# Short-sequence attention on one core: output held in SBUF until unit 34, four q and k buffers, the v wait on ScalarE, a placed loop head

## The chip, the cores and the metric

The kernel runs on one core of a Trainium2 chip. Time is device time in microseconds (us). The kernel before has a median of 143.16 us over nine runs. One execution was profiled: it took 142.82 us, of which the profile's span covers 140.7 us.

## The reference

There are 32 x 12 = 384 heads, each of sequence length 128 and head size 64, all float32.

```python
scale = 1.0 / np.sqrt(q.shape[-1])
scores = scale * np.matmul(q, k.transpose(0, 1, 3, 2))
scores_max = np.max(scores, axis=-1, keepdims=True)
attn = np.exp(scores - scores_max)
attn = attn / (np.sum(attn, axis=-1, keepdims=True) + 1e-8)
return np.matmul(attn, v).astype(np.float32)
```

q, k and v are drawn with a standard deviation of 0.1, so the scores are small and the kernel takes the exponential without subtracting the maximum.

## The kernel before, in words

The heads form 48 units of eight. Four units share one load of q and one of k (a "super", 12 in all) and one load of v (a "group", 12 in all). Each load reads 1 MiB of float32 and lands in SBUF as 512 KiB of bf16. The cast is made by the DMA, and all 36 loads are issued by GpSimd in one fixed order (`pool_load`): v of a group, then q and k of the next super.

TensorE runs a loop of seven trips over eight steps each (`tensor_program`). A step u has up to four parts: T, the transposes that bring q and k into head-major form; V, the matmuls with a selection matrix that put v's rows in order; S, the scores of unit u + 1; and O, the values of unit u. Unit m of v is reordered at step m - 3. The first and last trips skip the parts whose unit doesn't exist, with a branch on the trip number. Code outside TensorE is unrolled.

Between them the other engines work as follows. VectorE makes the pair tile for a transpose two steps ahead (P, `pair_up`), copies the transposed result out of PSUM (E, `keep_qk`) and normalises (N: a reciprocal and a multiply that writes `o_sb`). In a step its order is N, E, P. ScalarE copies each reordered v out of PSUM with a column of ones beside it (K, `keep_v`), then takes the exponentials (X, `exps`). SyncE issues the stores in order of the units. Everything is ordered by semaphores: each operation lists what it depends on, and a wait is placed in front of it.

Four places matter for the change.

- **The stores.** Output goes through ten buffers (`NO`), each of two units. Store c waits until the unit 14 after its last is normalised, but never beyond unit 36 (`LATE`, `LOADED`, line 373). The normalise that reuses a buffer waits for the store that used it ten before (line 346). Most stores are two DMAs.
- **The q and k buffers.** There are eight of each (`NQ`). A load waits for the pairs that read the buffer it overwrites (line 389).
- **The wait for v.** There are two v buffers (`NVB`), so group g may be issued only when the last unit of group g - 2 has been reordered (line 379). The landing of a group is waited for by VectorE, at the pair tile made for the step of the group's first reorder (line 330). TensorE's reorder in turn waits for that pair tile (line 297), and for the ScalarE copy of the unit before.
- **The loop head.** The loop on TensorE starts wherever the code ahead of it ends (line 493).

```python
        last = first + n - 1
        op("SP", ("store", c), emit, [("N", max(last, min(last + LATE, LOADED)))])
```

Of the kernel before, what the change touches and what calls it, by code (L numbers as in the profile page):

```python
# [10 lines left out]
def kernel(  # L11
# [7 lines left out]
    nc = tc.nc  # L19
    f32 = mybir.dt.float32  # L20
# [3 lines left out]
    B, H, S, D = q.shape  # L24
# [7 lines left out]
    NU = B * H // 8  # L32
# [32 lines left out]

    PERIOD = 8
    TRIPS = NU // PERIOD + 1


# [7 lines left out]
        v_at[m - 3] = [m]  # L79
    steps = range(min(t_at) - 2, NU + 1)  # L80

    NQ, NVB, NVE, NP, NT, NA, NO = 8, 2, 8, 4, 2, 4, 10

    LATE, LOADED = 14, NU - 12

    def sb(name, shape, dtype):
        return ctx.enter_context(nc.sbuf_tensor(name, shape, dtype))
# [11 lines left out]
    pair = [sb(f"pair{i}", [128, 8, 2, D], bf16) for i in range(NP)]  # L99
    qkT = [sb(f"qkT{i}", [128, 2, 16, S], bf16) for i in range(NT)]  # L100
    attnT = [sb(f"attnT{i}", [128, 2, 4, S], bf16) for i in range(NA)]
    o_sb = [sb(f"o_sb{i}", [128, 2 * 2 * RO * D], f32) for i in range(NO)]
    recip = [sb(f"recip{i}", [128, 2, RO], f32) for i in range(2)]
    qk_ps = ps("qk_ps", [128, 8 * S], bf16)
    s_ps = [ps(f"s_ps{i}", [128, 2, 4 * S], f32) for i in range(2)]
# [17 lines left out]
    def op(engine, key, emit, deps=(), marks=(), dma=()):  # L123
        o = Op()
        o.key, o.emit, o.deps, o.marks, o.dma = key, emit, deps, marks, dma
        assert key not in position, key
        position[key], engine_of[key] = len(program[engine]), engine
        program[engine].append(o)
# [101 lines left out]
    def keep_v(m):  # L230
        return nc.scalar.copy(v_e[m % NVE][:, :, :D], v_ps[:].rearrange("p (n e) -> p n e", e=D))  # L231
# [27 lines left out]
    def normalise(u):  # L259
        c, w, n, first = splace[u]  # L260
        o4 = o_ps[:, :, :RO * (D + 1)].rearrange("p a (r e) -> p a r e", e=D + 1)
        r = recip[u % 2]
        nc.vector.reciprocal(r[:], o4[:, :, :, D]).then_inc(s_r, 1)  # L263
        nc.vector.wait_ge(s_r, u + 1)
        o = o_sb[c % NO][:, :n * 2 * RO * D].rearrange("p (a w e) -> p a w e", a=2, w=n)
        return nc.vector.tensor_mul(  # L266
            o[:, :, w, :].rearrange("p a (r d) -> p a r d", d=D),
            o4[:, :, :, :D],
            r[:].unsqueeze(3).to_broadcast([128, 2, RO, D]))
# [6 lines left out]
    s_q = [tc.alloc_semaphore(f"s_q{i}") for i in range(NQ)]  # L276
    s_k = [tc.alloc_semaphore(f"s_k{i}") for i in range(NQ)]
    s_v = [tc.alloc_semaphore(f"s_v{i}") for i in range(NVB)]
    s_o = [tc.alloc_semaphore(f"s_o{i}") for i in range(NO)]
    v_readers = {}  # L280
    for u in range(NU):
        for a in range(2):
# [10 lines left out]

    def pe_order_v(m):

        g, w, n, first = vplace[m]
        deps = [("K", m - 1)] + ([("P", t_at[vstep_of[m]][0])] if w == 0 else [])
        op("PE", ("V", m), lambda: order_v(m), deps, ["pe_act"])

    def pe_scores(u):  # L300
        s = of_unit[u]
# [5 lines left out]
    def pe_values(u):  # L307
# [2 lines left out]
        deps.append(("N", u - 1))  # L310
        op("PE", ("O", u), lambda: values(u), deps, ["pe_dve"])

    def act_keep(m):
        deps = [("V", m)]
        if m >= NVE:
            deps += [("O", u) for u in v_readers[m - NVE]]
        op("ACT", ("K", m), lambda: keep_v(m), deps, ["act_pe"])

    def act_exps(u):
        deps = [("S", u)] + ([("O", u - NA)] if u >= NA else [])  # L320
# [2 lines left out]
    def dve_pair(t):  # L323
        s, j, b = t
        deps = [("T", t_order[t_index[t] - NP])] if t_index[t] >= NP else []
        dma = [((s_q, s_k)[j][s % NQ], 16 * (s // NQ + 1))]
        for m in v_at.get(t_step[t], []):
            g, w, n, first = vplace[m]
            if w == 0:
                dma.append((s_v[g % NVB], 16 * (g // NVB + 1)))  # L330
        op("DVE", ("P", t), lambda: pair_up(t), deps, ["dve_io"] if t_index[t] else ["dve_pe", "dve_io"], dma)

    def dve_keep(t):
# [7 lines left out]

    def dve_normalise(u):
        c, w, n, first = splace[u]
        dma = []
        if w == 0 and c >= NO:
            dma.append((s_o[c % NO], sum(16 * pieces(x) for x in range(c % NO, c, NO))))

        marks = ["dve_pe"] + (["dve_io"] if u + 8 > t_step[t_order[-1]] else [])
        op("DVE", ("N", u), lambda: normalise(u), [("O", u)], marks, dma)

    def pieces(c):

        first = sum(stores[:c])
        return 2 if 1 < stores[c] < supers[of_unit[first]][0] // 4 else 1

    def sp_store(c):
        n = stores[c]
        first = sum(stores[:c])
        R, f = supers[of_unit[first]]
        J = R // 4  # L360

        def emit():
            dst = o_rows[:, 2 * f:2 * f + 2 * J, :].rearrange("p (a w) e -> p a w e", a=2)[
                :, :, first - f:first - f + n, :]
            src = o_sb[c % NO][:, :n * 2 * RO * D].rearrange("p (a w e) -> p a w e", a=2, w=n)
            if pieces(c) == 1:
                nc.sync.dma_start(out=dst, in_=src).then_inc(s_o[c % NO], 16)
            else:
                for a in range(2):
                    nc.sync.dma_start(out=dst[:, a], in_=src[:, a]).then_inc(s_o[c % NO], 16)  # L370

        last = first + n - 1
        op("SP", ("store", c), emit, [("N", max(last, min(last + LATE, LOADED)))])

    def pool_load(kind, x):
        deps = []
# [19 lines left out]
        op("POOL", ("load", kind, x), emit, deps)  # L396


    op("ACT", ("K", -1), lambda: nc.scalar.drain(), [], ["act_pe"])
    at_step = {}  # L400
    for u in steps:
        start = len(program["PE"])
# [68 lines left out]
    def tensor_program():  # L471

        ops, waits, when = {}, {}, {}
        for o in program["PE"]:
            place = at_step[o.key] % PERIOD, o.key[0]
            w = waits_of("PE", o)
            assert waits.setdefault(place, w) == w and not o.dma, (o.key, w, waits[place])
            when.setdefault(place, []).append((at_step[o.key] // PERIOD + 1, o.emit is None))
            if at_step[o.key] // PERIOD == 2:
                ops[place] = o  # L480
        places = []
        for place in [(l, kind) for l in range(PERIOD) for kind in "TVSO"]:
            trips = [t for t, empty in when[place] if not empty]
            assert trips in (list(range(TRIPS - 1)), list(range(1, TRIPS))), (place, trips)
            waiting = len(when[place]) > len(trips)
            assert not waiting or len(when[place]) == TRIPS
            skipped = 0 if trips[0] else TRIPS - 1
            if waiting or not places or places[-1][0] != skipped:
                places.append((skipped, waits[place] if waiting else [], []))
            places[-1][2].append((ops[place], [] if waiting else waits[place]))  # L490
        trip = ctx.enter_context(nc.tensor.register("trip"))
        nc.tensor.reg_mov(trip, 0)
        with nc.tensor.Fori(0, TRIPS):
            for skipped, always, some in places:
                run_waits("PE", always)
                with nc.tensor.If_ne(trip, skipped):
                    for o, w in some:
                        run("PE", o, w)
            nc.tensor.reg_add(trip, trip, 1)

    with nc.Block() as block:
        @block.gpsimd
        def _(_e):
            for i, o in enumerate(program["POOL"]):
                if i == 2:
                    nc.gpsimd.wait_ge(s_zero, 1)
                    nc.gpsimd.affine_select(  # L507
                        out=ident[:], in_=ident[:], compare_op=mybir.AluOpType.not_equal,
                        fill=1.0, base=0, pattern=[[-1, 128]], channel_multiplier=1,
                    ).then_inc(s_id, 1)  # L510
                run("POOL", o, waits_of("POOL", o))

        @block.tensor
        def _(_e):
            tensor_program()

        @block.scalar
        def _(_e):
            for o in program["ACT"]:
                run("ACT", o, waits_of("ACT", o))  # L520

        @block.vector
        def _(_e):
            for t in sel.values():
                nc.vector.memset(t[:], 0.0)  # L525
            nc.vector.memset(ident[:], 0.0).then_inc(s_zero, 1)
            for t in v_e:
                nc.vector.memset(t[:, :, D:D + 1], 1.0)
            nc.vector.wait_ge(s_id, 1)

            for jv in range(2):
                nc.vector.tensor_copy(  # L532
                    sel[16][:].rearrange("p h v (x y s) -> p h v x y s", x=2, y=2)[:, :, jv, :, jv, :],
                    ident[:].rearrange("p (h s x) -> p h x s", h=8, x=2))
            for o in program["DVE"]:
                run("DVE", o, waits_of("DVE", o))

        @block.sync
        def _(_e):
            for o in program["SP"]:  # L540
                run("SP", o, waits_of("SP", o))
            for i in range(NO):
                nc.sync.wait_ge(s_o[i], sum(16 * pieces(x) for x in range(i, len(stores), NO)))


# [28 lines left out]
```

## Time and profile before

| what | value |
|---|---|
| median of the runs | 143.16 us (142.47 to 148.13) |
| profiled execution, its span | 142.82 us, 140.7 us |
| TensorE matmul busy | 99.3 us (71%) |
| VectorE busy | 90.1 us (64%) |
| ScalarE busy | 74.3 us (53%) |
| GpSimd's DMA queue (loads) | 18.88 MB, 76.8% of 16 engines |
| SyncE's DMA queue (stores) | 12.59 MB, 28.2% of 16 engines |
| instruction fetch of one queue | 4 transfers, 0.07 MB |
| granted TensorE clock, mean | 0.914 |

The DMA figures count bytes on the SBUF side. Packets overlap on an engine, so a share can be over 1. A busy row for TensorE overlaps its own weight loads. A wait is listed with the engine and tile that ended it; "issue" is idle time for which the profile shows no wait, and "PEq" is TensorE's sequencer.

### The profile page before, as it was taken

The numbers are of one execution on the slowest core, as the hardware profiler recorded it, in microseconds if no ns is written. First come the engines' busy times: TensorE is split into PE (matmuls) and PEld (weight loads), VectorE is DVE, ScalarE is ACT, GpSimd is POOL, SyncE is SP. The second block draws the span as 40 slices with busy tenths as digits, with TensorE's granted clock in tenths as the row PEclk, the third lists the DMA queues.
The fourth block names the chain that finished last, engine by engine and source line by source line (L and its number), as shares of the span: only waits on it lengthen the run. The fifth ranks groups of instructions, "written<-read, shape, count | busy, mean of one in ns | idle before, by whom it ended". The sixth has DMA issues, their size and how long they took to land. (4 is left out here: it accounts for less than half of the span.)

```text
span 140.7 us, 6998 instructions
## 1 busy us (share of the span) xinstructions
PE 99.3 (71%) x3072; PEld 70.1 (50%) x3072; DVE 90.1 (64%) x204; ACT 74.3 (53%) x97; POOL 27.0 (19%) x41
## 2 busy tenths in 40 slices
PE   0052939999859799885896797797694498597410
PEld 0042626677646566653574574475463366465310
DVE  2143623999599597965874973964964785685640
ACT  3000207778748848676357278077373448469700
POOL 6910002305060320602302302301500200000000
PEclk9999995999999999999779789689999959999955
DMA  2999999899999999999999999999999999999981
GB/s 17 187 201 211 208 206 177 138 200 183 178 184 160 212 186 192 209 180 236 243 235 239 251 237 240 252 235 242 253 231 240 255 226 311 379 373 369 327 302 61
DMA packets 25928, 31.55 MB, mean 224 GB/s; under 512 B 1345, under 2 KB 19777, under 8 KB 25921
## 3 DMA queue, kind: packets, MB, share of 16 engines
q0 software_dynamic: 12864, 18.88, 76.8%
q1 hardware_dynamic: 13056, 12.59, 28.2%
q8 instruction: 4, 0.07, 0.2%
q14 instruction: 4, 0.02, 0.0%
HBM read 37.75 MB, written 12.58 MB: 358 GB/s over the span
## 5 line engine op out<-in xcount | busy, mean ns | idle before, releaser
L231 ACT CAST v_e<-v_ps 128x512 bf16<-128x512 f32 x48 | 28.2, 588 | 57.7 <-PE v_ps L185 57.7
L236 ACT ACTIVATE attnT<-s_ps 128x1024 bf16<-128x1024 f32 x48 | 49.4, 1029 | 0.3 <-PE s_ps L211 0.2
L171 PE MATMUL qk_ps<-ident,pair 128*128 128x128 bf16 x384 | 33.4, 238 | 15.8 <-PEq L458 15.0
L254 DVE COPY qkT<-qk_ps 128x1024 bf16<-128x1024 bf16 x48 | 32.8, 684 | 4.6 <-PE qk_ps L171 3.5
L171 PEld LDWEIGHTS qk_ps<-ident,pair 128*128 128x128 bf16 x384 | 25.0, 106 | 20.8 <-issue 19.5
L185 PE MATMUL v_ps<-v_b,sel 128*32 128x256 bf16 x768 | 33.2, 297 | 2.9 <-issue 2.1
L266 DVE TENSOR_TENSOR o_sb<-o_ps,recip 128x512 f32<-128x512 f32 x48 | 33.2, 692 | 1.7
L223 PE MATMUL o_ps<-v_e,attnT 128*32 128x65 bf16 x1536 | 21.9, 202 | 16.5 <-PEq L458 16.3
L223 PEld LDWEIGHTS o_ps<-v_e,attnT 128*32 128x32 bf16 x1536 | 16.2, 101 | 22.6 <-issue 19.9
L381 POOL DMA_DIRECT2D v_b<-in_v_dram x12 | 9.5, 788 | 82.2 <-PE v_ps L185 82.2
L245 DVE COPY pair<-k_b 128x1024 bf16<-128x1024 bf16 x24 | 10.7, 446 | 20.0 <-DMA v_b<-in_v_dram 20.0
L185 PEld LDWEIGHTS v_ps<-v_b,sel 128*32 128x32 bf16 x768 | 17.2, 101 | 9.7 <-issue 4.9
L211 PE MATMUL s_ps<-qkT 64*128 64x128 bf16 x384 | 20.5, 231 | 0.6 <-PEq L458 0.5
L263 DVE RECIPROCAL recip<-o_ps 128x8 f32<-128x8 f32 x48 | 9.8, 203 | 13.2 <-PE o_ps L223 7.8
L211 PEld LDWEIGHTS s_ps<-qkT 64*128 64x128 bf16 x384 | 11.7, 99 | 11.6 <-issue 11.6
L245 DVE COPY pair<-q_b 128x1024 bf16<-128x1024 bf16 x24 | 10.4, 433 | 3.7 <-DMA q_b<-in_q_dram 3.6
L393 POOL DMA_DIRECT2D q_b<-in_q_dram x12 | 8.7, 724 | 1.0 <-SPq L92 1.0
L393 POOL DMA_DIRECT2D k_b<-in_k_dram x12 | 8.9, 738 | 0.0
L231 ACT ACT_TABLE_LOAD x1 | 1.3, 1283 | 1.0 <-SPq L92 1.0
L532 DVE COPY sel<-ident 128x128 bf16<-128x128 bf16 x2 | 0.4, 224 | 1.7 <-POOL ident L507 1.7
L525 DVE MEMSET sel<- 128x256 uint32 x1 | 0.3, 272 | 1.1 <-SPq L92 1.1
L507 POOL TENSOR_SCALAR_AFFINE_SELECT ident<-ident 128x128 bf16<-128x128 bf16 x1 | 0.3, 313 | 0.1
(6 smaller groups left out, 0.8 us busy)
## 6 DMA issues: line engine op xcount, KB each, us to landing
out_dram<-o_sb SPq DMA_DIRECT2D x48, 256.0 KB, 7.1
q_b<-in_q_dram POOLq DMA_DIRECT2D x12, 512.0 KB, 11.4
k_b<-in_k_dram POOLq DMA_DIRECT2D x12, 512.0 KB, 13.6
v_b<-in_v_dram POOLq DMA_DIRECT2D x12, 512.0 KB, 9.8
```

The costliest lines, as they stand in the source:

```text
L171: i = nc.tensor.transpose(p[:, :, r4, jj, :], x[:, r].rearrange("p a d -> p (a d)"), ident[:])
L185: x = nc.tensor.matmul(t[r4 * 32:(r4 + 1) * 32, i, :, :], lhsT=pick[:, w * nh + i, jv, :], rhs=v_b[g % NVB][:, :n, (4 * jv + r4) * D:(4 * ...
L211: i = nc.tensor.matmul(t[:, a, h, :], lhsT=x[p, 1, 4 * w + h, :], rhs=x[p, 0, 4 * w + h, :], start=True, stop=True)
L223: y = nc.tensor.matmul(t[h * SO:(h + 1) * SO, a, r * (D + 1):(r + 1) * (D + 1)], lhsT=x[:, a, h, r * SO:(r + 1) * SO], rhs=v_e[m % NVE][:, ...
L231: return nc.scalar.copy(v_e[m % NVE][:, :, :D], v_ps[:].rearrange("p (n e) -> p n e", e=D))
L236: return nc.scalar.activation(out=attnT[u % NA][:].rearrange("p a h (r s j) -> p (a h r) s j", r=4, j=J), in_=s_ps[u % 2][:].rearrange("p ...
L245: return nc.vector.tensor_copy(pair[t_index[t] % NP][:], src[:, 8 * b:8 * b + 8])
L254: return nc.vector.tensor_copy(x.rearrange("p h (r j s) -> p (h r) j s", r=4, j=J)[:, :, 2 * b:2 * b + 2, :].rearrange("p x j s -> p x (j ...
L263: nc.vector.reciprocal(r[:], o4[:, :, :, D]).then_inc(s_r, 1)
L266: return nc.vector.tensor_mul(o[:, :, w, :].rearrange("p a (r d) -> p a r d", d=D), o4[:, :, :, :D], r[:].unsqueeze(3).to_broadcast([128, ...
L381: op("POOL", ("load", kind, x), lambda: nc.gpsimd.dma_start(out=v_b[x % NVB][:, :n, :], in_=v_rows[:, first:first + n, :],).then_inc(s_v[x ...
L393: nc.gpsimd.dma_start(out=bufs[x % NQ][:], in_=rows[R][:, n:n + 2, :]).then_inc(sm[x % NQ], 16)
```

## The change

The output buffers become one per store, the whole output in SBUF (26 tiles, 96 KiB per partition). Each store waits for its own last unit or for unit 34, whichever is later, so nothing is stored before unit 34 and then all held stores follow at once. The normalise waits for no store. q and k have four buffers each in place of eight.

The wait for a group of v moves from VectorE to ScalarE. The copy K of the unit before a group's first (for the first group, a drain) now also waits for that group's landing, and TensorE's reorder waits for that copy alone.

The loop on TensorE is built with a set place of its first instruction: slot 108 of a block in which instructions are fetched. The code ahead of it branches over the padding.

```diff
-    PERIOD = 8
+    PERIOD, FIRST = 8, -8
...
-    NQ, NVB, NVE, NP, NT, NA, NO = 8, 2, 8, 4, 2, 4, 10
-
-    LATE, LOADED = 14, NU - 12
+    NQ, NVB, NVE, NP, NT, NA = 4, 2, 8, 4, 2, 4
+
+    HELD = NU - 14
...
-    o_sb = [sb(f"o_sb{i}", [128, 2 * 2 * RO * D], f32) for i in range(NO)]
+    o_sb = [sb(f"o_sb{c}", [128, n * 2 * RO * D], f32) for c, n in enumerate(stores)]
...
-        g, w, n, first = vplace[m]
-        deps = [("K", m - 1)] + ([("P", t_at[vstep_of[m]][0])] if w == 0 else [])
-        op("PE", ("V", m), lambda: order_v(m), deps, ["pe_act"])
+        op("PE", ("V", m), lambda: order_v(m), [("K", m - 1)], ["pe_act"])
...
+    def v_landing(m):
+        if m == NU or vplace[m][1]:
+            return []
+        g = vplace[m][0]
+        return [(s_v[g % NVB], 16 * (g // NVB + 1))]
+
     def act_keep(m):
...
-        op("ACT", ("K", m), lambda: keep_v(m), deps, ["act_pe"])
+        op("ACT", ("K", m), lambda: keep_v(m), deps, ["act_pe"], v_landing(m + 1))
...
-        for m in v_at.get(t_step[t], []):
-            g, w, n, first = vplace[m]
-            if w == 0:
-                dma.append((s_v[g % NVB], 16 * (g // NVB + 1)))
...
-        if w == 0 and c >= NO:
-            dma.append((s_o[c % NO], sum(16 * pieces(x) for x in range(c % NO, c, NO))))
...
-        op("SP", ("store", c), emit, [("N", max(last, min(last + LATE, LOADED)))])
+        op("SP", ("store", c), emit, [("N", max(last, HELD))])
...
-    op("ACT", ("K", -1), lambda: nc.scalar.drain(), [], ["act_pe"])
+    op("ACT", ("K", -1), lambda: nc.scalar.drain(), [], ["act_pe"], v_landing(0))
...
-        with nc.tensor.Fori(0, TRIPS):
+        with nc.Fori(
+                0, TRIPS, engines=bass.OrderedEngineSet([nc.tensor.engine]),
+                head_slot={nc.tensor.engine: 108}):
```

The rest of the diff is bookkeeping that follows from these: semaphores of the stores counted by four, and the trip of a step counted from step -8, which gives the same trips as before.

More of the change, by code (lines that the diff above doesn't have):

```diff
@@ L264, in normalise @@
         nc.vector.wait_ge(s_r, u + 1)
-        o = o_sb[c % NO][:, :n * 2 * RO * D].rearrange("p (a w e) -> p a w e", a=2, w=n)
+        o = o_sb[c][:].rearrange("p (a w e) -> p a w e", a=2, w=n)
         return nc.vector.tensor_mul(
@@ L278 @@
     s_v = [tc.alloc_semaphore(f"s_v{i}") for i in range(NVB)]
-    s_o = [tc.alloc_semaphore(f"s_o{i}") for i in range(NO)]
+    s_o = [tc.alloc_semaphore(f"s_o{i}") for i in range(4)]
     v_readers = {}
@@ L343, in dve_normalise @@
         c, w, n, first = splace[u]
-        dma = []
-        if w == 0 and c >= NO:
-            dma.append((s_o[c % NO], sum(16 * pieces(x) for x in range(c % NO, c, NO))))
         marks = ["dve_pe"] + (["dve_io"] if u + 8 > t_step[t_order[-1]] else [])
-        op("DVE", ("N", u), lambda: normalise(u), [("O", u)], marks, dma)
+        op("DVE", ("N", u), lambda: normalise(u), [("O", u)], marks)
     def pieces(c):
@@ L364, in emit @@
                 :, :, first - f:first - f + n, :]
-            src = o_sb[c % NO][:, :n * 2 * RO * D].rearrange("p (a w e) -> p a w e", a=2, w=n)
+            src = o_sb[c][:].rearrange("p (a w e) -> p a w e", a=2, w=n)
             if pieces(c) == 1:
-                nc.sync.dma_start(out=dst, in_=src).then_inc(s_o[c % NO], 16)
+                nc.sync.dma_start(out=dst, in_=src).then_inc(s_o[c % 4], 16)
             else:
                 for a in range(2):
-                    nc.sync.dma_start(out=dst[:, a], in_=src[:, a]).then_inc(s_o[c % NO], 16)
+                    nc.sync.dma_start(out=dst[:, a], in_=src[:, a]).then_inc(s_o[c % 4], 16)
         last = first + n - 1
-        op("SP", ("store", c), emit, [("N", max(last, min(last + LATE, LOADED)))])
+        op("SP", ("store", c), emit, [("N", max(last, HELD))])
     def pool_load(kind, x):
@@ L474, in tensor_program @@
         for o in program["PE"]:
-            place = at_step[o.key] % PERIOD, o.key[0]
+            trip, l = divmod(at_step[o.key] - FIRST, PERIOD)
+            place = l, o.key[0]
             w = waits_of("PE", o)
             assert waits.setdefault(place, w) == w and not o.dma, (o.key, w, waits[place])
-            when.setdefault(place, []).append((at_step[o.key] // PERIOD + 1, o.emit is None))
-            if at_step[o.key] // PERIOD == 2:
+            when.setdefault(place, []).append((trip, o.emit is None))
+            if trip == 2:
                 ops[place] = o
@@ L541, in _ @@
                 run("SP", o, waits_of("SP", o))
-            for i in range(NO):
-                nc.sync.wait_ge(s_o[i], sum(16 * pieces(x) for x in range(i, len(stores), NO)))
+            for i in range(4):
+                nc.sync.wait_ge(s_o[i], sum(16 * pieces(x) for x in range(i, len(stores), 4)))
 _INS = ['q', 'k', 'v']
```

## The prediction

> **What bounds the kernel now.** I read the slices first, then stages cut at the landings of v, then the waits, then the timeline around one landing. The two rows of the page's slices (40 slices of 3.5 us):
>
> ```profile
> DMA  2999999899999999999999999999999999999981
> GB/s 17 187 201 211 208 206 177 138 200 183 178 184 160 212 186 192 209 180 236 243 235 239 251 237 240 252 235 242 253 231 240 255 226 311 379 373 369 327 302 61
> ```
>
> The DMA engines are full from the second slice to the last but one, yet at three rates: about 200 GB/s while only loads run, 240 with stores among them, 370 with stores alone. So the end is set by transfers. The stages (columns: start and end, us, busy of five engines with counts, clock, DMA share, GB/s):
>
> ```profile
> 4.00:24.00 20.00, 10.71 (x144) 7.16 (x148) 7.38 (x14) 3.33 (x6) 3.98 (x7) 0.92 1.15 207
> 24.00:26.00 2.00, 2.00 (x92) 1.52 (x88) 1.48 (x4) 1.39 (x2) 1.83 (x3) 0.94 0.33 47
> 26.00:38.90 12.90, 12.42 (x444) 9.04 (x428) 10.77 (x25) 10.26 (x15) 2.23 (x3) 1.00 1.11 189
> 38.90:55.70 16.80, 13.76 (x495) 10.00 (x490) 14.26 (x33) 11.76 (x16) 4.36 (x6) 1.00 1.09 185
> 55.70:120.60 64.90, 50.97 (x1561) 35.80 (x1560) 44.45 (x97) 36.70 (x49) 11.90 (x16) 0.89 1.13 242
> 120.60:130.00 9.40, 7.00 (x280) 4.98 (x278) 7.14 (x15) 6.66 (x10) 0.00 (x0) 1.00 1.08 373
> 130.00:138.80 8.80, 2.41 (x128) 1.64 (x112) 3.60 (x8) 2.92 (x3) 0.00 (x0) 0.70 0.83 284
> ```
>
> Three losses are to be seen. At 24 to 26 us the DMA nearly stops (share 0.33). From 26 to 55.7 us loads alone run at 187 (the byte-weighted mean of 189 and 185), where the first eight, all queued at once, ran at 207. From 130 us stores run at 284, not 373, because they wait for the last units. The waits:
>
> ```profile
> POOL v_b L381 <- PE v_ps L185: 82.2, 10, 16.0
> DVE pair L245 <- DMA v_b<-in_v_dram: 20.0, 11, 2.7
> DVE recip L263 <- DMA out_dram<-o_sb: 5.1, 5, 2.2
> ```
>
> GpSimd may issue a group of v only when TensorE has reordered the last unit of the group two before; VectorE waits for each landing; five times it waits for an output buffer. The timeline, at the start and around the landing of the fourth group of v:
>
> ```profile
> 20.26 0.62 PE L185 MATMUL v_ps<-v_b,sel 128*32 128x256 bf16 x15 [2.13 <-issue]
> ...
> 23.68 0.74 POOL L381 DMA_DIRECT2D v_b<-in_v_dram  x1 [16.02 <-PE v_ps L185]
> ...
> 38.94 0.43 DVE L245 COPY pair<-k_b 128x1024 bf16<-128x1024 bf16 x1 [1.84 <-DMA v_b<-in_v_dram]
> 39.07 0.75 POOL L381 DMA_DIRECT2D v_b<-in_v_dram  x1 [5.43 <-PE v_ps L185]
> ...
> 40.35 0.43 PE L223 MATMUL o_ps<-v_e,attnT 128*32 128x65 bf16 x32 [1.27 <-PEq L458]
> ```
>
> TensorE stops 2.13 us in the middle of a reorder, with no semaphore named; the third v is issued at 23.68, as the queue runs dry; at 38.94 VectorE, freed by a landing, lets the values matmul go 1.4 us later.
>
> **The ledger of before.** Loads are 18.88 MB in SBUF (12 groups of q, k, v, 1.573 MB each), stores 12.59 MB. By 55.7 us the rows have moved 4.14 + 0.09 + 2.44 + 3.11 = 9.78 MB of loads; 9.10 remain. The mixed stage moved 64.9 x 242 = 15.7 MB, so 6.6 MB were stores, 17.7 us at the 373 of stores alone; the loads there had 47.2 us, or 193 GB/s. Transfers end near 138.75, the span at 140.7, the profiled execution at 142.82. The median, 143.16, is 0.34 above it; 1% (1.4 us) is about what a measurement of this kernel tells from no change.
>
> **Stores held to unit 34.** Nothing is taken off the DMA: the same 48 stores, 12.59 MB, 33.75 us at 373. [...] By the rows, what can change is how full the engines are when loads run alone (187 against 193), and the slack at the end. In the last 8.8 us 284 x 8.8 = 2.50 MB moved, 6.7 us at 373: 2.1 us of slack. All units will be done long before the last store, so this goes, but for a ragged finish of the DMA engines that I put at 0.7 (0 to 2). The issuing work on SyncE is covered: two issues of one store were 0.41 us apart in the trace, a half store takes 0.35 us at 373, and the queue starts beside loads. If that cover is gone, 27 further issues cost 0.06 each, 1.6 us at most. The five output waits (5.1 us on VectorE) go, and with them five waits of SyncE's issue order; they lay beside loads, so 0.
>
> **q and k in 4 buffers.** q and k of the next super are issued right behind a v that waits for TensorE; the pairs that read the buffer four back were made over ten steps before. Cost 0; the v gate covers it, and if q were gated it would show as a new GpSimd wait on pair.
>
> **The v wait from VectorE to ScalarE.** VectorE's pair at two steps ahead no longer waits for v. Now the copy of the unit before each group waits for the landing, with that step's exponential queued behind it on ScalarE; TensorE stops at the group's first reorder, behind that copy. After a landing: copy 0.59, reorder 0.62, three steps of 1.85 (transposes began at 24.35 and 35.47, six steps), some 0.3 of handoffs: the gate of the next v opens 7.1 us after the landing. In before it took 9.06 and 9.21 (38.94 to the issue at 48.00, 47.62 to 56.83). So each v is issued some 2 us sooner after a landing. With landings 8.2 us apart that is 1.1 us ahead of the next landing rather than 0.1 to 0.4 behind it. The exponential behind the wait ends at 0.1 + 0.59 + 1.03 = 1.7, about when TensorE has passed reorder and scores (1.6), so 0 to 0.2 per group, off the path as long as 7.4 us of compute per group is under the landing interval. What it buys is a deeper queue: bounds are 187 (no better than before alone) and 207 (the queue always deep). I take 191, nearer 187, because not all of the shortfall need be dry queue: the DMA share at 187 was still 1.09 to 1.11.
>
> **The start, and the loop head.** The first k pair no longer waits for the first v (2.69 us on VectorE), so the reorders start near 12.3 instead of 14.09, and are then paced by q at 15.5 and k at about 18. The fourth reorder ends near 20.7 if TensorE doesn't stop, and near 23 if it does. [...] The first trip takes branches over parts whose units don't exist yet. [...] Then v is issued near 21, the lag from issue to flow is about 2 us (23.68, and 47 GB/s until 26), and the stop at 24 to 26 goes: 0.32 MB, 1.5 us, which if kept comes back whole.
>
> **The sum.** Transfers end at 24 + (18.88 - 4.14) MB / r + 33.75 + 0.7. At r = 191 that is 24 + 77.2 + 34.45 = 135.6, 3.1 before 138.75; 142.82 - 3.1 = 139.7 us.
>
> **Rivals.**
> Start stop kept, loads no better than alone before: r = 187, 78.8 us, plus 1.5: 142.8. For it: the unexplained part of 187; against it, two waits ahead of the start are removed. No measurable change.
>
> The queue of loads starves: loads alone lose to the gate on v_b what stores filled in the mixed stage. The place is each switch from k to v between 26 us and the release; the price is r for 14.74 MB. Shorter stages show how low it goes: 176 in 37.5 to 46.1 us. At 176: 83.75 us, 146.3. It is slower than before from r under 184, by over 1% under 180. For it: two thirds of the loads now have no stores beside them. Against it: the 2 us earlier gate.
>
> Held stores crowd out the last loads. Unit 34 comes at about 24 + 11.6 MB / 0.191 + 4.7 = 89, with 2.25 MB of loads left. At 120 GB/s (half of the 242) they take 19 us; the last eight units' compute, 13 us more, is done at 122, 12 before the stores. It decides only where loads get under about 70 GB/s. Stores wholly first would mean about 150. The mixed stage gave loads 9.10 of 15.7 MB, which speaks against it.
>
> Queue always deep: r = 207, 71.2 us, 133.7.
>
> **Chances.** Forecast (r 187 to 197: 141.3 to 137.3) 0.56; start stop kept, no change 0.17; starved loads 0.14; crowded last loads 0.03; deep queue 0.10. Faster by over 1% of the median (under 141.7; r over 186): 0.66; within 1% 0.17; slower 0.17. The range, 136.5 to 145.0, leaves out the ends of starved and deep.
>
> **What would show it.** Slices near 190 GB/s until about 89 us, then a mixed stretch, then 370 to the end; no slice near 138 at 25 us; ScalarE's copies waiting for v, VectorE's pairs not; v issued about 7 us after each landing; no wait on o_sb; the last normalise many us before the last landing. Wrong if loads alone fall under 184 GB/s, if TensorE's stop moves to where v's third issue waits for it, or if pure stores in long runs drop below 373.

## The result and the profile after

The change takes 140.31 us (median of 10 runs, 138.70 to 142.93). The kernel before, run beside it, took 143.36 us (31 runs). The ratio is 0.976, with an interval of 0.972 to 0.980. The forecast was 139.7. Ratios here are of the faster executions alone (those within 1.5% of the fastest of the same kernel), so that a ratio can differ from the quotient of two medians, and the profiled execution of the change, 141.31 us with a span of 139.2, is not among them. Where its rates matter, a row of e1 stands beside it: the change without the placed loop head, an execution of 139.62 us.

The slices of the page of the change (40 slices of 3.5 us):

```profile
DMA  2999999699999999999999999999999999999992
GB/s 16 183 198 211 208 212 189 95 203 176 184 205 143 193 208 211 205 206 213 187 204 182 203 192 210 197 157 214 244 260 374 382 380 377 354 363 349 347 340 91
```

Loads run alone to about 91 us, a short mixed stretch follows, then stores alone. Two things don't fit the forecast: the slice of 95 near 25 us is still there, and the stores fall from 380 to between 340 and 363 in the last five full slices. The stages (columns as for before: start and end, us, busy of five engines with counts, clock, DMA share, GB/s):

```profile
4.00:24.00 20.00, 9.55 (x126) 6.44 (x128) 7.15 (x14) 4.09 (x6) 3.65 (x6) 0.95 1.14 207
24.00:26.00 2.00, 2.00 (x64) 1.58 (x58) 0.98 (x3) 1.43 (x2) 1.85 (x3) 0.65 0.24 36
26.00:91.00 65.00, 61.05 (x2140) 44.11 (x2132) 59.74 (x133) 50.17 (x67) 17.81 (x25) 1.00 1.13 194
91.00:104.00 13.00, 10.71 (x376) 7.72 (x376) 10.84 (x24) 8.79 (x12) 0.74 (x1) 1.00 1.13 219
104.00:120.00 16.00, 10.80 (x399) 7.56 (x392) 8.61 (x18) 9.62 (x12) 0.00 (x0) 0.82 1.09 375
120.00:136.90 16.90, 0.25 (x19) 0.09 (x7) 0.90 (x2) 0.00 (x0) 0.00 (x0) 0.50 1.02 343
```

Loads alone run at 194 GB/s to 91 us; 191 was forecast. The 187 of before is of a shorter stretch, since its stores begin near 55 us. In that stretch the rows of before, of the change and of e1 are:

```profile
26.00:55.70 29.70, 26.18 (x931) 19.04 (x916) 25.03 (x58) 22.01 (x30) 6.59 (x9) 1.00 1.10 187
```

```profile
26.00:55.70 29.70, 27.61 (x972) 19.90 (x960) 27.21 (x61) 22.68 (x30) 6.90 (x10) 1.00 1.11 188
```

```profile
26.00:55.70 29.70, 27.68 (x965) 20.02 (x963) 27.08 (x62) 22.68 (x31) 7.14 (x10) 1.00 1.13 195
```

In this stretch the profiled change gains next to nothing. Its third group of v comes late, and the granted clock was 0.50 from 22.0 to 25.4 us, where that group is released. e1 had a clock of 1.00 through all of its loads and runs at 195 here, at 196 to 91 us. The waits:

```profile
POOL v_b L378 <- PE v_ps L185: 67.5, 10, 16.5
ACT v_e L231 <- DMA v_b<-in_v_dram: 7.7, 5, 3.2
DVE pair L245 <- DMA q_b<-in_q_dram: 6.5, 5, 3.0
```

GpSimd waits 15 us less for the reorders. ScalarE waits for v five times, besides 12.2 us for the first landing. VectorE waits for v no more, but for q five times (before, twice, 3.6 us). Nothing waits for an output buffer. The timeline gives the time from a landing to the issue of the next v but one:

```profile
71.21 0.59 ACT L231 CAST v_e<-v_ps 128x512 bf16<-128x512 f32 x1 [0.87 <-DMA v_b<-in_v_dram]
...
79.10 0.82 POOL L378 DMA_DIRECT2D v_b<-in_v_dram  x1 [5.73 <-PE v_ps L185]
```

It is 7.9 us, where before it was 9.1 to 9.2; by the landings in the trace it is 8.0 to 8.2 in the last six groups. At the start the same view shows two transposes of TensorE's first trip and the third v, and the view of the loop's branch shows how long the branches took (least, median, most, ns), here and, in the last line, before:

```profile
14.79 1.01 PE L171 MATMUL qk_ps<-ident,pair 128*128 128x128 bf16 x8 [4.27 <-PEq L455]
...
20.33 0.61 PE L171 MATMUL qk_ps<-ident,pair 128*128 128x128 bf16 x8 [1.62 <-PEq L455]
...
24.15 0.75 POOL L378 DMA_DIRECT2D v_b<-in_v_dram  x1 [16.49 <-PE v_ps L185]
...
L498 PEldq COMPARE_BRANCH  x84: 63/63/4949, 1.5 to 118.2; - x84
```

```profile
L496 PEldq COMPARE_BRANCH  x84: 63/63/342, 1.2 to 133.2; - x84
```

The pair tile for the transpose at 14.79 was made by 9.7 and the copy it waits for by 11.3, so most of the idle 4.27 us is not for data: a branch of 4.95 us, begun at 9.55, lies there, and one of 2.34 us ahead of the transpose at 20.33. Before, no branch took more than 0.34 us, and the one stop was 2.13. The third v is issued at 24.15, no sooner than the 23.68 of before. (In e8, which has the same program for TensorE and a clock of 1.00 there, it is issued at 23.51.)

### The profile page after: what moved, and what is told of

Same layout as the page of the kernel before. It is cut to its first block, busy times and chain, and to the rows that moved or that the text cites. A ratio compares the mean times of both kernels' runs of the same rounds, so it can differ in the third digit from the quotient of the medians.

```text
span 139.2 us, 6979 instructions
## 1 busy us (share of the span) xinstructions
PE 94.3 (68%) x3072; PEld 67.5 (48%) x3072; DVE 89.2 (64%) x204; ACT 74.1 (53%) x97; POOL 26.7 (19%) x41
## 3 DMA queue, kind: packets, MB, share of 16 engines
q0 software_dynamic: 12864, 18.88, 78.5%
## 5 line engine op out<-in xcount | busy, mean ns | idle before, releaser
L231 ACT CAST v_e<-v_ps 128x512 bf16<-128x512 f32 x48 | 28.2, 588 | 31.6 <-PE v_ps L185 23.6
L171 PE MATMUL qk_ps<-ident,pair 128*128 128x128 bf16 x384 | 32.0, 231 | 18.0 <-PEq L455 17.6
L171 PEld LDWEIGHTS qk_ps<-ident,pair 128*128 128x128 bf16 x384 | 23.9, 103 | 22.6 <-issue 21.2
L185 PE MATMUL v_ps<-v_b,sel 128*32 128x256 bf16 x768 | 31.5, 287 | 4.1 <-PEq L455 4.1
L185 PEld LDWEIGHTS v_ps<-v_b,sel 128*32 128x32 bf16 x768 | 16.8, 99 | 10.3 <-issue 5.7
L211 PE MATMUL s_ps<-qkT 64*128 64x128 bf16 x384 | 19.5, 223 | 0.6 <-PEq L455 0.5
L211 PEld LDWEIGHTS s_ps<-qkT 64*128 64x128 bf16 x384 | 11.1, 96 | 10.9 <-issue 10.9
L245 DVE COPY pair<-k_b 128x1024 bf16<-128x1024 bf16 x24 | 10.2, 427 | 0.0
L231 ACT ACT_TABLE_LOAD x1 | 1.3, 1283 | 12.2 <-DMA v_b<-in_v_dram 12.2
```

The costliest lines, as they stand in the source:

```text
L171: i = nc.tensor.transpose(p[:, :, r4, jj, :], x[:, r].rearrange("p a d -> p (a d)"), ident[:])
L185: x = nc.tensor.matmul(t[r4 * 32:(r4 + 1) * 32, i, :, :], lhsT=pick[:, w * nh + i, jv, :], rhs=v_b[g % NVB][:, :n, (4 * jv + r4) * D:(4 * ...
L211: i = nc.tensor.matmul(t[:, a, h, :], lhsT=x[p, 1, 4 * w + h, :], rhs=x[p, 0, 4 * w + h, :], start=True, stop=True)
L245: return nc.vector.tensor_copy(pair[t_index[t] % NP][:], src[:, 8 * b:8 * b + 8])
```

## The experiments

All ratios are to the kernel before, timed beside each run on the same chip.

**The parts of the change, two by two.** Without the placed loop head (e1):

```diff
-        with nc.Fori(
-                0, TRIPS, engines=bass.OrderedEngineSet([nc.tensor.engine]),
-                head_slot={nc.tensor.engine: 108}):
+        with nc.tensor.Fori(0, TRIPS):
```

> The change without the placed loop head; all else as in the change. The profile of the change shows two branches of TensorE's first trip that last 4.95 and 2.34 us, and the third v issued at 24.15 us, so the start stop of the DMA is still there. Theory (the slot moved TensorE's stop onto the way to the third v and costs): without it the branches take under 0.4 us, one stop of about 2.1 us comes back in the third reorder, the third v is issued at 22 to 23 us, and the time is 0.5 to 1.5 us under the change (138.8 to 139.8). Rival (the slot is worth something or nothing): equal to the change within 0.3 us or above it (140.3 or more).

Measured: 139.69 us, ratio 0.977 (0.969 to 0.985), the same as the change. The long branches are gone (the longest 0.34 us) and the stop inside the third reorder is back, with a stop of 1.01 us in the first:

```profile
20.03 1.04 PE L185 MATMUL v_ps<-v_b,sel 128*32 128x256 bf16 x15 [1.89 <-issue]
...
23.68 0.75 POOL L378 DMA_DIRECT2D v_b<-in_v_dram  x1 [16.02 <-PE v_ps L185]
```

So in the change the slot moves TensorE's stop and is worth nothing that can be measured. By the ratios the rival's "equal" holds. The time lies in the range of the theory, but its third v at 22 to 23 us did not come, and before ran a little faster beside this run too (143.12 us).

The wait for v back on VectorE, all else as in the change (e2), and the same without the placed loop head, so that held stores and four buffers alone are left (e3):

```diff
-        op("PE", ("V", m), lambda: order_v(m), [("K", m - 1)], ["pe_act"])
+        g, w, n, first = vplace[m]
+        deps = [("K", m - 1)] + ([("P", t_at[vstep_of[m]][0])] if w == 0 else [])
+        op("PE", ("V", m), lambda: order_v(m), deps, ["pe_act"])
...
-        op("ACT", ("K", m), lambda: keep_v(m), deps, ["act_pe"], v_landing(m + 1))
+        op("ACT", ("K", m), lambda: keep_v(m), deps, ["act_pe"])
...
+        for m in v_at.get(t_step[t], []):
+            dma += v_landing(m)
...
```

> The change with the wait for v put back on VectorE; stores held, four buffers and the loop head stay. Theory (the wait on ScalarE lets the next v be issued sooner and keeps the queue of loads deeper): loads alone fall from the 194 GB/s of the change to about 187, v is issued about 9 us after a landing that was waited for, and the time is 1.5 to 2.5 us over the change (about 142). Rival (the place of the v wait is worth nothing, since the DMA engines are full either way): within 0.5 us of the change.

> Only the held stores and the four q and k buffers; the v wait on VectorE and the loop head as in the kernel before. Theory (the gain comes from loads at a better rate and the slack at the end, and the first needs the moved wait): loads alone at 187 GB/s, start stop kept, 1.4 us of slack gone: 142 to 143, about 1 us or less under before. Rival (holding the stores is the whole gain): as the change, 140.3 within 0.5.

Measured: e2 144.05 us (ten executions, 142.13 to 145.91), ratio 1.001 (0.996 to 1.007); e3 146.45 us, ratio 1.022 (1.014 to 1.030). The stages from 26 to 91 us, e2 first, then e3, and one landing and the issue that it allows in e2:

```profile
26.00:91.00 65.00, 57.14 (x2000) 41.20 (x1984) 55.49 (x124) 46.93 (x64) 15.68 (x23) 1.00 1.10 190
```

```profile
26.00:91.00 65.00, 56.94 (x1906) 40.95 (x1904) 53.33 (x120) 44.97 (x60) 15.96 (x22) 0.95 1.09 184
```

```profile
46.58 0.43 DVE L245 COPY pair<-k_b 128x1024 bf16<-128x1024 bf16 x1 [0.51 <-DMA v_b<-in_v_dram]
...
55.82 0.75 POOL L382 DMA_DIRECT2D v_b<-in_v_dram  x1 [5.79 <-PE v_ps L185]
```

Loads alone run at 190 and 184, against 194 in the change and 196 in e1. In e2 the issue comes 9.2 us after the landing, 9.1 to 9.5 in all groups from the third on. Held stores with the wait on VectorE are no gain at all, and without the placed loop head they are a loss: this is the starving queue that the prediction had as its slower rival. The theory of e2 had the rate and the interval nearly right and the loss too small; the theory of e3 had put it at a small gain; both rivals fall.

Only the loop head lies between e2 and e3, 2% by the ratios, but it is not shown that the slot makes the difference. In e3's profile the granted clock was 0.50 for 3.4 us twice in this stage (the row has 0.95, that of e2 1.00), and the four intervals from landing to issue in and after these stretches are 10.3 to 10.7 us, the others after the start 9.1 to 9.4. Yet an execution of e3 at 146.75 us had the mean clock of e2's profile, 0.916. It was not tried further.

The moved wait and nothing else, on the kernel before (e5; the edit of e2 the other way round):

> The kernel before with the wait for v moved to ScalarE and nothing else. Theory (the moved wait is the gain, whatever the stores do): 140 to 141.4, the third v near 22.5 to 23.7 us, loads alone at about 195 GB/s. Rival (it pays only with held stores, since held stores alone lost 2.2% and the moved wait brought the held kernel from 146 to 140): stores among loads already fill the gaps, so 142 to 143.

Measured: 140.68 us, ratio 0.985 (0.972 to 0.998). So the moved wait gains alone: 193 GB/s from 26 to 55.7 us, where before had 187, though the third v, at 24.12, came no sooner. Its executions had a mean granted clock of 0.967 to 0.971, those of before beside them 0.912 to 0.950; but executions of before with 0.962 and 0.968 (beside e1) took 142.00 and 143.22 us, so the clock alone does not make the gain. And the change with the stores released as before (e4):

```diff
-        op("SP", ("store", c), emit, [("N", max(last, HELD))])
+        op("SP", ("store", c), emit, [("N", max(last, min(last + 14, NU - 12)))])
```

> The change, but each store released as in the kernel before (14 units after its last, none beyond unit 36); the whole output still has its own room, so no wait for a buffer. Theory (stores and loads add up wherever they lie, and holding buys the slack at the end, 2.1 us less a ragged finish): 1 to 2 us over the change, about 141.5. Rival (stores among loads fill the gaps of a queue of loads that runs dry, so the mixed stage is worth as much): within 0.5 us of the change.

Measured: 141.39 us, ratio 0.980 (0.970 to 0.991). The time is that of the theory, but the ratio can't be separated from that of the change. Its mixed slices run at 229 to 245 GB/s and its last full slices of stores alone at 380. The table, without the placed loop head:

| | v wait on VectorE | v wait on ScalarE |
|---|---|---|
| stores as before | 1.000 | 0.985 (0.972 to 0.998) |
| stores held | 1.022 (1.014 to 1.030) | 0.977 (0.969 to 0.985) |

The upper row has eight q and k buffers and the ten shared output buffers, the lower has the change's. The moved wait is worth 1.5% with stores among the loads and 4.5% with stores held. Holding costs 2.2% on the left; on the right the intervals overlap.

**Is it a queue that runs dry?** In the change the third v stands behind a wait for TensorE, and with it everything after it on GpSimd. One edit puts q and k of one group more ahead of that wait (e6):

```diff
-            loads.append((t_step[s, j, 0] - 2, "qk"[j], s))
+            loads.append((t_step[s, j, 0] - 6, "qk"[j], s))
```

> The change with every load of q and k issued one group earlier in GpSimd's order, so that the fourth q and k stand ahead of the third v, which waits for TensorE. Theory (after 24 us and up to about 45 us the queue of loads runs dry, because the third v is issued too late): no slice under 150 GB/s at 25 us, loads alone at 200 or more, 1.5 to 3 us under the change: 137.3 to 138.8. Rival (the slow stretches are not a dry queue): within 0.5 us of the change.

Measured: 137.32 us, ratio 0.966 (0.962 to 0.970), beside 0.976 (0.972 to 0.980) of the change. The slices and the stage of loads alone:

```profile
GB/s 14 172 213 210 204 210 201 212 207 209 208 209 211 207 212 206 212 208 211 207 210 213 205 211 207 211 208 203 228 211 372 379 381 378 362 350 345 343 345 108
...
26.00:91.00 65.00, 62.57 (x2192) 45.45 (x2192) 61.40 (x137) 52.16 (x69) 16.64 (x23) 1.00 1.16 209
```

The slow slices at 25 us and up to 45 us are gone, and loads run at 209 to the end, although the third v is issued at 24.31, as late as ever. So those stretches were a dry queue; a full one gave 209 here, and 207 from 4 to 24 us in before and in the change.

The same with the wait for v put back on VectorE (e10):

> q and k one group ahead and stores held, with the wait for v put back on VectorE. Theory (the moved wait pays because it makes v's issue earlier against a queue that runs dry): with two more loads queued at the start less of it is needed, but v is still issued about 9 us after a landing that was waited for while a group takes 7.5 us, so the loads fall behind again: 190 to 200 GB/s, 139 to 141. Rival (a deeper queue alone is enough): 137.3 within 0.5.

Measured: 146.83 us, the median of four executions from 144.19 to 147.87, which scatter too much for an interval. The fastest lies within the range of before (142.09 to 144.41), so a loss against before is not shown; but all four are 5% or more over the slowest of e6 (137.37). So more loads at the start are not enough: the gain of e6 needs the moved wait. In the profiled execution (147.23 us) the loads run at 186 from 26 to 91 us. The timelines show the two cases, first e6, then e10:

```profile
32.91 0.59 ACT L231 CAST v_e<-v_ps 128x512 bf16<-128x512 f32 x1 [0.68 <-DMA v_b<-in_v_dram]
...
40.44 0.59 ACT L231 CAST v_e<-v_ps 128x512 bf16<-128x512 f32 x1 [0.82 <-DMA v_b<-in_v_dram]
40.50 0.76 POOL L378 DMA_DIRECT2D v_b<-in_v_dram  x1 [5.49 <-PE v_ps L185]
...
47.94 0.59 ACT L231 CAST v_e<-v_ps 128x512 bf16<-128x512 f32 x1 [0.54 <-DMA v_b<-in_v_dram]
```

```profile
34.10 0.43 DVE L245 COPY pair<-k_b 128x1024 bf16<-128x1024 bf16 x1 [1.80 <-DMA v_b<-in_v_dram]
...
43.54 0.76 POOL L382 DMA_DIRECT2D v_b<-in_v_dram  x1 [7.26 <-PE v_ps L185]
...
50.98 0.43 DVE L245 COPY pair<-k_b 128x1024 bf16<-128x1024 bf16 x1 [1.80 <-DMA v_b<-in_v_dram]
```

With two buffers for v, two groups pass in the time from a landing to the issue that it allows, plus the time from that issue to its landing. In e6 these are 7.6 (32.91 to 40.50) and 7.4 us (40.50 to 47.94): 15.0 for two groups, 7.5 for one, and 1.573 MB / 7.5 us is 210 GB/s; the stage shows 209. In e10 they are 9.4 and 7.4: 8.4 for one, 187 GB/s; the stage shows 186. That the sums give the rates is no test, since exactly two groups land in that time whatever sets it. What the runs show is which term differs: the first is 9.1 to 9.6 us with the wait on VectorE (e2, e10) and 7.5 to 8.2 with it on ScalarE (e1, e6), once the start is over, while the second stays between 7.0 and 8.7 up to the last group.

The kernel before with the early q and k alone (e12, the same edit):

> The kernel before with only the loads of q and k one group earlier in GpSimd's order. Theory (the start stop and the slow stretch to 45 us are a dry queue, about 1.5 and 1.5 us; the v wait on VectorE then still holds v's issue back, but stores fill those gaps): 140 to 141. Rival (the order of loads pays only together with the moved wait and the held stores): 142.5 or more.

Measured: 146.89 us, ratio 1.031 (1.018 to 1.043). The theory falls. With q and k ahead of it the first v lands at 17.8 instead of 11.9, and the wait on VectorE holds up the pairs of k behind which all else is queued; the third v then goes out at 29.16:

```profile
17.89 0.43 DVE L245 COPY pair<-k_b 128x1024 bf16<-128x1024 bf16 x1 [8.37 <-DMA v_b<-in_v_dram]
...
29.16 0.76 POOL L381 DMA_DIRECT2D v_b<-in_v_dram  x1 [20.00 <-PE v_ps L185]
```

```profile
GB/s 13 186 211 203 207 210 205 211 77 205 201 168 200 171 187 205 209 230 188 225 239 242 239 241 244 237 242 242 238 243 247 259 81 290 380 380 379 376 309 8
```

The slow slice has only moved on, to about 30 us, and another is near 116 us, behind the last v, which is issued at 113.70. With the wait on ScalarE (e6) the first landing is as late, 17.8 us, but it holds up the first copy alone, and the pairs of k go on.

Early q and k with the stores as before (e9, the edits of e6 and e4):

> q and k one group ahead, as in the run before that kept loads at 209 GB/s (137.3 us), but each store released as in the kernel before. Theory (with a queue of loads that is never dry, loads and stores add up wherever the stores lie): equal to the held kernel within 1 us, 136.5 to 138; the stores at the end run at 380 GB/s rather than 343, but wait for the last units. Rival (holding the stores is worth something of its own): 1.5 us or more over it, about 139.

Measured: 138.46 us, ratio 0.965 (0.952 to 0.977). It can't be told from e6's 0.966: holding the stores is not what gains, once the loads are fed.

**The slot, and TensorE's stops in the first trip.** Slot 110, with four semaphore increments at the head of the loop (e7):

```diff
-                head_slot={nc.tensor.engine: 108}):
+                head_slot={nc.tensor.engine: 110}):
+            for _ in range(4):
+                nc.tensor.sem_inc(s_spare, 1)
```

> The change with the loop head at slot 110 and four small semaphore increments at the head of the loop, so that the instruction on which TensorE waits before its first transpose is the first of a fetch block. [...]

Measured: 144.16 us, ratio 1.011 (1.002 to 1.020).

```profile
L501 PEldq COMPARE_BRANCH  x84: 63/63/4149, 2.1 to 120.0; - x84
```

The longest branches are 4.15 and 2.37 us, and the time is 3.9 us over that of the change: the moved loop head does not take the long branches away. The trace lists the increments at 51 ns each. In this execution the first q also landed 0.9 us later, so that the first transpose begins at 8.71 instead of 7.61 and the third v goes out at 25.31. Loads alone fall to 188 GB/s, and from 40 us on the issue of v comes 8.3 to 8.8 us after a landing, where the last six groups of the change have 8.0 to 8.2. Whether the increments lengthen this interval, and how much of the 3.9 us comes of it, is not shown.

The trace also lists the transfers of the instruction queue, four of 16 KB that took 0.9 to 1.0 us each in the change. There the second and third end at 13.14 and 18.53 us and the long branches at 14.50 and 20.04; here the transfers end at 13.45 and 18.87, the branches at 14.81 and 20.37; before, the third ends at 18.70 and the stop at 20.26. So these five stops end 1.4 to 1.6 us after the end of such a transfer. That they wait for it is a reading of these times alone, since no record names what ends them. What makes a transfer begin is open. The second to fourth begin at 12.2, 17.6 and 23.3 us in the change, at 12.0, 17.8 and 23.8 before and at 12.5, 18.0 and 23.6 here, nearly the same times wherever the loop head lies; but in e12, where TensorE stood until 19 us, at 12.0, 23.5 and 28.8. In the first three the stop stays near the same times, and it is a branch that stands there in the change and here, a reorder before.

**Why stores alone slow down.** Half of the two-part stores issued by GpSimd (e8):

```diff
-                for a in range(2):
-                    nc.sync.dma_start(out=dst[:, a], in_=src[:, a]).then_inc(s_o[c % 4], 16)
+                nc.sync.dma_start(out=dst[:, 0], in_=src[:, 0]).then_inc(s_o[c % 4], 16)
...
+            nc.gpsimd.dma_start(out=dst[:, 1], in_=src[:, 1]).then_inc(s_second, 16)
```

> The change with the second half of each two-part store issued by GpSimd, not by SyncE. In the profile of the change SyncE issues a store of 256 KB every 0.77 us from 120 us on (343 GB/s), and ends last. Theory (SyncE's issue bounds the last 17 us): these run at 375 GB/s or more, and the time is 1 to 1.6 us under the change: about 139. Rival (the DMA engines bound it, at a lower rate for stores alone): the rate stays at 343 and the time within 0.5 us.

Measured: 140.74 us, ratio 0.990 (0.981 to 0.998).

```profile
104.00:112.00 8.00, 5.86 (x232) 4.08 (x232) 4.56 (x11) 7.01 (x10) 5.44 (x8) 1.00 1.04 397
112.00:120.00 8.00, 2.29 (x112) 1.64 (x112) 3.29 (x7) 2.39 (x3) 0.78 (x2) 0.68 1.02 351
120.00:128.00 8.00, 0.00 (x0) 0.00 (x0) 0.00 (x0) 0.00 (x0) 0.00 (x0) 0.50 1.03 341
```

The stores of GpSimd took 11.3 us from issue to landing in the median. By the issues and landings of the trace 15 stores were under way at 116 us and 11 at 120, where the change ran at 380 with 8 or 9; and the rate fell to about 345 nonetheless. So SyncE's issue is unlikely to be the bound, though the change alone would suggest it: there the stores under way fall from 8 at 116 us to 5 at 122, as the rate falls. By its ratio this kernel is 1.4% slower than the change. And the kernel of e6 with idle engines kept busy to the end (e11), by work whose results nobody reads:

```diff
+            for n in range(64):
+                if n > 1:
+                    nc.tensor.wait_ge(s_busy, n - 1)
+                nc.tensor.matmul(
+                    s_ps[0][:, n % 2, :], lhsT=ident[:],
+                    rhs=qkT[0][:, 0, 0:4, :].rearrange("p h s -> p (h s)"), start=True, stop=True).then_inc(s_busy, 1)
...
+            for n in range(14):
+                if n:
+                    nc.scalar.wait_ge(s_idle, n)
+                nc.scalar.activation(
...
```

> q and k one group ahead, stores held, and behind the program 64 more matmuls on TensorE and 14 more exponentials on ScalarE, whose results nobody reads, so that these engines and the clock stay busy while the stores drain. In the held kernels the stores fall from 380 to about 343 GB/s near the time at which compute ends; with stores as before they stay at 380 to the end. Theory (the rate falls because the core goes idle): 375 to 380 through most of the drain and about 1.3 us under the same kernel without the extra work (136). Rival (the rate falls after some 14 us of stores alone, whatever the engines do): 343 again and 137.3 within 0.5.

Measured: 138.23 us, ratio 0.968 (0.959 to 0.977).

```profile
104.00:112.00 8.00, 6.11 (x258) 4.26 (x258) 4.63 (x11) 6.70 (x10) 0.00 (x0) 1.00 1.09 380
112.00:118.00 6.00, 3.87 (x80) 1.76 (x81) 2.61 (x6) 5.86 (x7) 0.00 (x0) 0.72 1.06 366
118.00:124.00 6.00, 6.00 (x28) 2.56 (x27) 0.00 (x0) 5.81 (x7) 0.00 (x0) 1.00 1.03 345
```

With the clock at 1.00 and two engines busy the rate is 345, as without. An idle core is not the cause. Nor is a fixed time shown: by the slices stores alone hold about 380 for 11 us in e2, 14 in the change, 18 in e3 and 20 in e1 before they fall. The cause stays open.

## Why the prediction was right, and where it was not

The time came out within 0.6 us, in part by luck: the rate of the loads was better than forecast, the start and the drain were worse. Of the three signs that I had named for being wrong two came true, TensorE's stop at the third v and long stores under 373. The ledger of the profiled change, in the form of the sum: loads left at 26 us are 18.88 - 4.14 - 0.07 = 14.67 MB, at 194 GB/s 75.6 us; that ends at 101.6. The stores took 33.75 us in the sum; at 375 and 343 the stages of 104 to 136.9 us moved 6.00 + 5.80 = 11.8 MB in 32.9 us, where 373 gives 31.6, so 35.05. With the 0.7 that the sum has for the ragged finish the transfers end at 137.4; the last store landed at 137.6. The sum had 135.6; 1.0 of the 1.8 us between them is what the profiled execution lies over its median.

- **What bounds it: right.** With stores held, a run's time follows the rate of loads alone and the rate of stores; TensorE's busy share is beside the point, but its pace sets the issue of v.
- **The v wait: right, and the largest part.** The interval from landing to issue fell from 9.1 to 7.9 us (forecast 7.1). The missing 0.8 are the three steps, 6.1 us between the reorders at 72.07 and 78.16 and not 5.55, with VectorE now waiting for q among them, and handoffs of 0.7 and not 0.3. The rate was 194 (forecast 191, bounds 187 and 207). It was less even than forecast: in the profiled change about 180 up to 48 us, 205 to 71, 197 to 91. What I called "a deeper queue" is the cycle of two buffers, and e2 and e10 beside e1 and e6 show that the moved wait shortens its first term. The "0.1 to 0.4 behind" of before left out its next landing, where the issue was 1.2 us behind (55.67 and 56.83). What I left out is the start: the issue of v lags from 24 us on, and the gap lasts to 45 us. e6 shows the bound of 207 is there to be had.
- **Stores held: the sign of its own part was wrong.** I argued that held stores buy 2.1 us of slack less 0.7. Alone they lost 2.2% (e3), and beside the moved wait their worth can't be measured. With the loads fed it made no difference where the stores lay (e9 0.965, e6 0.966), so their worth there is nearer 0 than my 1.4 us. The ledger could not show that, since its 193 was worked out with the 373 taken as given. The slack is gone as forecast, but stores alone then ran at 343 for half of the drain (1.3 us), and the loads lost the stores that filled their gaps.
- **The start: wrong.** The sum counts nothing for a stop of TensorE, and no run shows that 0. What the runs showed in its place: before and e1 stop for 2.13 and 1.89 us without a long branch, and in the change the stop of 2.13 became two branches of 4.95 and 2.34 us, the third v went out at 24.15, and the stop of the DMA stayed (36 GB/s against 47), the 1.5 us that I had said would come back whole. The trace of before could not show it. The reorders did begin where forecast without the placed slot, at 12.48 us in e1.
- **q and k in 4 buffers: nothing contradicts 0.** No wait of GpSimd on a pair is in the profile after. It was not tried alone.
- **The ragged finish (0.7) and SyncE's issue (0 to 1.6): not settled.** The 0.7 was my estimate, and no run shows it by itself: in the change the engines were busy for a share of 0.65 from 136 to 137 us and of 0.03 in the half us after that. The fall to 343 is of that size; e8 speaks against SyncE's issue as its cause, and none is shown.
- **Rivals.** The starving queue came true in e3 (184 GB/s, the break-even that I had named, and 2.2% slower), not in the change. The crowding of the last loads did not come: v of the last group landed at 106.7 us and the last unit was normalised near 121, 16 us before the last store.

The best version found is the change with q and k issued one group earlier, at 0.966 of the kernel before with stores held (e6) and 0.965 without (e9).

## What to carry to other kernels

With two buffers two blocks of a stream pass in (landing to next issue + issue to landing). This holds by definition and predicts nothing by itself; but it tells where to look. Here a wait that was put one step later in the consumers' order shortened the first term by about 1.1 us, and how long that term is can be read off two lines of a timeline before any change. Held stores alone, beside loads at 184 GB/s, lost 2.2% (e3), and with loads at 206 to 209 GB/s from 26 to 48 us their place made no difference (e6, e9): feed the stream first, then ask whether the move is still worth anything. Put loads that need no permission ahead of the one that does, but only if no engine waits for that one in the middle of other work: the same reordering gained 1% in the change and lost 3% in the kernel before.

## What the runs showed of the hardware that was not expected

- Stores alone fell from 380 to about 345 GB/s after 11 to 20 us of a drain (e2, e1), with the core idle or busy (e6, e11), and with half of the stores issued by another engine (e8). In e4, where each store waited for its unit and stores ran alone for some 15 us, they kept 380 almost to the end.
- A branch of TensorE in the first trip of a loop lasted 4.95 us while loads ran at 198 to 211 GB/s, and ended 1.4 us after a transfer of 16 KB on the instruction queue had ended. The stop of before (2.13 us) ended 1.6 us after one, the two long branches of e7 (4.15 and 2.37 us) 1.4 and 1.5 us.
